# Router products from rows not yet normalised, and expert rows modulated on GpSimd, in a two-layer diffusion backbone

## The chip, the cores and the metric

The kernel runs on one core of a Trainium2 chip. The metric is the device time of one execution in microseconds, the median of several runs. A profiled execution of the kernel before gives the trace that is read here.

## What is computed

Two layers over 512 token rows of 1024 columns: 256 latent tokens and 256 context tokens, which have different modulation vectors. Each layer has three mixers (attention, gated linear attention, neighbourhood attention), merged by gates and an output product, and then a mixture of experts:

```
y  = w_out( sum_i sigmoid(gate_i(h)) * proj_i(branch_i) )
x  = LayerNorm(alpha * x + gate1 * y)
h2 = LN0(x) * (1 + scale2) + shift2
x  = LayerNorm(alpha * x + gate2 * HierMoE(h2))     # top-1 of 4 groups, then top-2 of its 8 experts
```

LN0 takes off a row's mean and divides by its deviation. The router multiplies h2 by a weight of 36 columns (4 for the groups, 32 for the experts) and adds a bias. The chosen experts get the rows of h2 and weight their results by the gates. The last layer needs the latent tokens alone.

## The kernel before

Rows are worked on in tiles of 128 tokens: four in layer 0 (tiles 0 and 1 latent, 2 and 3 context), two in layer 1. A modulation vector so belongs to a pair of tiles, s = t // 2. Products in full precision are put together from a high and a low part of each operand, three products in the place of one (`mm3`, L380 to L382).

`out_norm` ends the mixers. For each tile it makes the output products (PSUM tile wo, 48 products of 512 columns), multiplies them by the gate (L1107), adds them to the residual (L1108) and normalises (`norm1`, L354 and L355). L355 writes the rows x1 and their sums. `norm2` then makes the rows h2 of LN0 (`norm0`: statistics L300, factor by `rsqrt` L276 to L281, the row by ScalarE, L320), and `logits` transposes them (L1151), modulates the transposed tiles while it takes them out of PSUM (half on VectorE, L1159, half on ScalarE, L1157) and multiplies by the router's weight (L1161). `top2` adds the bias (L1200) and picks group and experts by a chain of small operations on 8 or 64 columns, up to the table M (L1223), two tiles at a time. `h2_done` transposes the modulated tiles back into token rows (L1126) and splits them into a high part on ScalarE and a low part on VectorE (L806, L807).

`route` then counts the rows of each expert (cum, rank, row) and makes one-hot matrices OH (L1362), with which `experts` gathers rows (XT, L1384) ahead of the first product with an expert's weight (L1507). Expert weights come as loads of 1 MB (`ew`, L1464). Between the mixers of layer 0 and its experts the modulation vector of layer 1 is also made (`modulation`, L493: sixteen loads of 512 KB named wmod, products L495).

The order on each engine is made by a scheduler that reads the program as written and places instructions by its own estimates; buffers are reused by tag, and a load waits until the last reader of its buffer is done. All loads named here are issued by SyncE (SP), in its order. GpSimd (POOL) does additions of the merge (L1046) and of the experts' results (L1433), and nothing between the two in either layer.

Of the kernel before, what the change touches and what calls it, by code (L numbers as in the profile page):

```python
# [23 lines left out]
EPS = 1e-6  # L24
# [68 lines left out]
HB = (), ()  # L93
LAST = 1, 0
# [12 lines left out]
QS = (2,), ()  # L107
# [142 lines left out]
class _Prog:  # L250
# [220 lines left out]
    def modulation(self, l, groups, tag="raw", tag2="b2", ps="mod"):  # L471
# [12 lines left out]
        for g in groups:  # L484
# [15 lines left out]
            nc.vector.tensor_tensor(mg, p, bm, op=ALU.add)  # L500
            pt = self.ps(ps + "T")
# [8 lines left out]
            for j in range(4):  # L510
                if g == 0:
                    o, plus = self.mT[l][:, 1 - j // 2], j // 2
                elif (g, j // 2) in ((1, 1), (2, 0)):
                    o, plus = self.mT2[l][:, 2 - g], g - 1
                else:
                    continue
# [536 lines left out]
    def out_norm(self, l, T, src):  # L1053
# [44 lines left out]
        for t in range(T):  # L1098
# [20 lines left out]
    def h2_done(self, l, t):  # L1119

        nc = self.nc
        hi, lo = self.t([128, 1024], "h4", F32R, "h2hi"), self.t([128, 1024], "h4", F32R, "h2lo")
        for i in range(2):
            p = self.ps("h2b")
            for k in range(4):
                nc.tensor.transpose(p[:, 128 * k:128 * k + 128], self.h2T[t][:, 4 * i + k], self.ident)  # L1126
            ns = slice(512 * i, 512 * i + 512)
            if t in HB[l]:
                x = self.t([128, 512], "b2", name="h2f")
                nc.scalar.copy(hi[:, ns], p)  # L1130
# [581 lines left out]
```

## Time and profile before

| | us |
|---|---|
| runs (3): median, lowest to highest | 2150.22, 2148.58 to 2153.83 |
| profiled execution, its own time | 2150.77 |
| its span in the trace | 2148.9 |
| TensorE busy in the span | 1973.0 |
| VectorE busy | 964.7 |
| ScalarE busy | 561.5 |
| GpSimd busy | 277.5 |

The span runs from the first to the last instruction; the 1.9 us beside it are start and end. The trace gives each instruction its start and length on its engine: PE is TensorE, DVE VectorE, ACT ScalarE, POOL GpSimd, SP SyncE. A busy TensorE is not one at its peak, since the ends of products are modelled. TensorE's mean granted clock was 0.969 of its full level. What is written behind a row in brackets is the idle time of the engine before it and what ended that.

### The profile page before, as it was taken

Reading aid. Unit: us, or ns where it says so; the run is one execution under the profiler, and the core shown is the slowest. Engines: PE = TensorE matmul, PEld = TensorE weight load, DVE = VectorE, ACT = ScalarE, POOL = GpSimd, SP = SyncE. Lnnn points to the kernel's source line nnn. Section 1 sums busy time; section 2 is a strip of 40 time slices with the busy share of each in tenths; the row PEclk is TensorE's granted clock in tenths of the full one; section 3 lists DMA queues with packets and bytes.
Section 4 is the critical chain, followed back from the end, with each engine's and each line's share of the span. In section 5 each row is a group of like instructions: output and inputs, shape, how many; then the busy total and the mean of one; then the engine's idle time right before and its main releaser. Section 6 shows DMA issues by size and latency. Waiting matters only on the chain. (4 is left out here: it accounts for less than half of the span.)

```text
span 2148.9 us, 28075 instructions
## 1 busy us (share of the span) xinstructions
PE 1973.0 (92%) x10749; PEld 1179.0 (55%) x10749; DVE 964.7 (45%) x2236; ACT 561.5 (26%) x992; POOL 277.5 (13%) x268
## 2 busy tenths in 40 slices
PE   6999999999998898989899598999996999999995
PEld 2676777767885353445253176887795433333331
DVE  4676765554487131222022766776658222221113
ACT  3453344443333000000010254444452111100000
POOL 1322100011100010111011222100020001000000
PEclk9999999999999999999999798999997999999998
DMA  8436222333328999999998723642466999999995
GB/s 300 160 118 220 69 69 70 94 99 120 99 91 321 400 420 420 372 385 420 420 369 367 276 84 116 197 127 85 140 210 253 401 421 422 422 422 422 421 422 224
DMA packets 113987, 562.41 MB, mean 262 GB/s; under 512 B 13302, under 2 KB 14838, under 8 KB 72120
## 3 DMA queue, kind: packets, MB, share of 16 engines
q1 hardware_dynamic: 113272, 558.85, 67.7%
q8 instruction: 87, 1.43, 0.3%
q10 hardware_dynamic: 576, 1.70, 0.2%
q14 instruction: 52, 0.43, 0.1%
HBM read 557.36 MB, written 3.15 MB: 261 GB/s over the span
## 5 line engine op out<-in xcount | busy, mean ns | idle before, releaser
L1507 PE MATMUL h<-ew,XT 128*64 128x512 f32 (+2 forms) x2048 | 479.0, 616 | 39.6 <-DMA ew<-in_ew_dram 39.5
L1507 PEld LDWEIGHTS h<-ew,XT 128*64 128x64 f32 (+2 forms) x2048 | 147.3, 136 | 325.7 <-issue 251.0
L1415 PE MATMUL Y<-ew,aT 128*64 128x512 f32 (+2 forms) x1024 | 250.4, 598 | 10.2 <-DMA ew<-in_ew_dram 7.8
L292 DVE TENSOR_TENSOR wlo<-raw,whi 128x1024 fp32r<-128x1024 f32 (+1 forms) x140 | 179.1, 1279 | 138.0 <-ACT whi L291 136.9
L1433 POOL TENSOR_TENSOR x<-x,ct 128x512 f32<-128x512 f32 x82 | 104.9, 1306 | 996.9 <-DVE ct L1432 873.7
L380 PE MATMUL pT<-hThi,whi 128*128 128x512 f32 (+1 forms) x576 | 204.0, 354 | 2.2 <-DVE zq L869 1.4
L291 ACT CAST whi<-raw 128x1024 fp32r<-128x1024 f32 (+1 forms) x140 | 145.4, 1039 | 223.4 <-PE pT L381 123.8
L382 PE MATMUL pT<-hThi,wlo 128*128 128x512 f32 (+1 forms) x576 | 203.2, 353 | 0.2 <-DVE wlo L292 0.2
L381 PE MATMUL pT<-hTlo,whi 128*128 128x512 f32 (+1 forms) x576 | 202.9, 352 | 0.0
L1404 DVE SCALAR_TENSOR_TENSOR act<-h,s,sl 128x512 f32<-128x512 f32 x30 | 22.5, 751 | 317.6 <-PE h L1507 263.9
L806 ACT CAST Yh<-Y 128x512 fp32r<-128x512 f32 x60 | 35.2, 586 | 467.7 <-PE Y L1415 467.7
L1415 PEld LDWEIGHTS Y<-ew,aT 128*64 128x64 f32 (+2 forms) x1024 | 75.5, 133 | 149.2 <-issue 123.8
L807 DVE TENSOR_TENSOR Yl<-Y,Yh 128x512 fp32r<-128x512 f32 x60 | 41.4, 690 | 252.8 <-ACT Yh L806 249.7
L380 PEld LDWEIGHTS pT<-hThi,whi 128*128 128x128 f32 x576 | 110.7, 192 | 23.8 <-issue 6.0
L382 PEld LDWEIGHTS pT<-hThi,wlo 128*128 128x128 f32 x576 | 110.7, 192 | 16.1 <-issue 2.6
L381 PEld LDWEIGHTS pT<-hTlo,whi 128*128 128x128 f32 x576 | 110.7, 192 | 14.3 <-issue 1.9
L380 PE MATMUL pM<-whi,hThi 128*128 128x512 f32 (+1 forms) x304 | 110.7, 369 | 3.6 <-ACT qTkT L645 1.9
L381 PE MATMUL pM<-wlo,hThi 128*128 128x512 f32 (+1 forms) x304 | 110.9, 365 | 0.0
L382 PE MATMUL pM<-whi,hTlo 128*128 128x512 f32 (+1 forms) x304 | 110.1, 364 | 0.0
L495 PE MATMUL mod<-wmod,sT 128*32 128x512 f32 x320 | 75.2, 636 | 22.5 <-DVE s L341 14.1
L1408 ACT COPY aT<-aT 128x512 f32<-128x512 f32 x30 | 17.6, 585 | 294.4 <-PE aT L1407 294.4
L1384 PE MATMUL XT<-OH,h2hi 128*128 128x256 f32 x352 | 88.6, 289 | 0.2 <-DVE OH L1362 0.2
(364 smaller groups left out, 3088.5 us busy)
## 6 DMA issues: line engine op xcount, KB each, us to landing
ew<-in_ew_dram SPq DMA_DIRECT2D x326, 1024.0 KB, 13.6
raw<-in_w_dram SPq DMA_DIRECT2D x145, 512.0 KB, 3.7
ew<-in_ew_dram SPq DMA_DIRECT2D x116, 512.0 KB, 13.5
wmod<-in_wmod_dram SPq DMA_DIRECT2D x96, 512.0 KB, 6.4
nb<-in_nb_dram SPq DMA_DIRECT2D x32, 256.0 KB, 3.8
g<-md SPq DMA_DIRECT2D x12, 256.0 KB, 7.3
row<-in_ln_dram SPq DMA_DIRECT2D x4, 512.0 KB, 5.3
lgb<-in_ln_dram SPq DMA_DIRECT2D x4, 512.0 KB, 12.2
```

The costliest lines, as they stand in the source:

```text
L291: self.nc.scalar.copy(hi, src)
L292: (eng or self.nc.vector).tensor_tensor(lo, src, hi.bitcast(F32), op=ALU.subtract)
L380: mm(out, lh, rh, start=start, stop=False)
L381: mm(out, lh, rl, start=False, stop=False)
L382: mm(out, ll, rh, start=False, stop=stop)
L495: nc.tensor.matmul(p[32 * j:32 * j + 32, :], self.sT[:, k, :], raws[j // 2][:, 512 * (j % 2):512 * (j % 2) + 512], start=k == 0, stop=k == 7)
L806: self.nc.scalar.copy(hi, src)
L807: self.nc.vector.tensor_tensor(lo, src, hi.bitcast(F32), op=ALU.subtract)
L1384: mm(p[:, w * j:w * j + w], self.h2s[t][part][:, 128 * k:128 * k + 128], OH[:, t], start=t == 0 and part == 0, stop=t == T - 1 and part == 1)
L1415: mm(y[m * i:m * i + m, :], aT[:, 128 * f + m * i:128 * f + m * i + m], w2(f, n, i), start=f == 0, stop=f == 3)
L1433: (nc.vector if last and n else nc.gpsimd).tensor_tensor(self.x1[t][:, ns], self.x1[t][:, ns], tmp, op=ALU.add)
L1507: mm(h[m * i:m * i + m, :], XTs[dp][:, k, 128 * pr + m * i:128 * pr + m * i + m], w[i, 2 * q + k // 4][k % 4], start=k == 0, stop=k == 7)
```

## The change

Four things change.

- `logits` transposes x1 as it is, ahead of the second norm, and takes it out of PSUM by two plain copies. The router's weight is multiplied by 1 + scale2 beforehand (`wrs`, two operations per pair). With mean m and factor r of a row, its logits are r times the product, minus r m times the column sums of wrs, plus the product of shift2 with the weight, plus the bias.
- `router`, a new function at the start of the output stage, makes wrs, the column sums (eight products with ones per pair, L1133) and the products with the shift (eight per pair, L1135). It is called ahead of the loads of the output weights.
- `top2` puts mean and factor in by two operations per tile (L1216, L1217), where one for two tiles added the bias.
- `h2` makes the experts' rows without transposes: four loads per pair bring scale and shift as rows to all partitions (`m2`, L1159), ScalarE squares and sums (L1165) and writes the normalised row (L1170), GpSimd multiplies and adds (L1174, L1175, two halves each), ScalarE writes the high part and GpSimd the low part (L288, L289). `h2_done` is gone. `modulation` stores scale2 with one added.

```diff
         def norm2(t):
             first[t]()
-            h = self.t([128, 1024], "o4", name="h2")
-            self.norm0(self.x1[t], h, total[t] if t in QS[l] else None)
-            self.logits(l, t, h)
-
+            self.logits(l, t, T)
+            self.h2(l, t, total[t])
+
+        self.router(l, T)
...
             norm1(t)
             norm2(t)
-            if t % 2 and t < T - 1:
+            if t % 2:
                 self.top2(l, t - 1, t + 1, T)
-            if t:
-                self.h2_done(l, t - 1)
-        if LAST[l]:
-            self.h2_done(l, T - 1)
-        self.top2(l, T - 2, T, T)
...
+    def router(self, l, T):
...
+        for s in range(T // 2):
+            ws = [self.t([128, 4, 36], "u1", name="wrs") for _ in range(2)]
+            for i in range(2):
+                nc.vector.tensor_tensor(ws[i], wr[:, 144 * i:144 * i + 144].rearrange("p (k e) -> p k e", e=36),
+                                        self.mT2[l][:, 0, s, 4 * i:4 * i + 4][:, :, None].to_broadcast([128, 4, 36]), op=ALU.mult)
+            self.wrs.append([ws[k // 4][:, k % 4] for k in range(8)])
+            o = 144 + 72 * s
+            for k in range(8):
+                mm(self.pl[:, o:o + 36], self.c["one"][:, 0:1].to_broadcast([128, 128]), self.wrs[s][k], start=k == 0, stop=k == 7)
+            for k in range(8):
+                mm(self.pl[:, o + 36:o + 72], self.mT2[l][:, 1, s, k:k + 1].to_broadcast([128, 128]), wr[:, 36 * k:36 * k + 36], start=k == 0, stop=k == 7)
+            nc.vector.tensor_tensor(self.brt[:, s], self.brt[:, s], self.pl[:, o + 36:o + 72], op=ALU.add)
+
+    def logits(self, l, t, T):
...
+            (nc.scalar.copy if i and t < T - 1 else nc.vector.tensor_copy)(xT[:, 4 * i:4 * i + 4], p.rearrange("p (a b) -> p a b", a=4))
         for k in range(8):
-            mm(self.pl[:, 36 * t:36 * t + 36], hT[:, k], self.wr[:, 36 * k:36 * k + 36], start=k == 0, stop=k == 7)
+            mm(self.pl[:, 36 * t:36 * t + 36], xT[:, k], self.wrs[t // 2][k], start=k == 0, stop=k == 7)
+
+    def h2(self, l, t, total):
...
+            for g, j in ((2, 0), (1, 2)):
+                for i in range(2):
+                    r = self.t([128, 512], "u2", name="m2")
+                    nc.sync.dma_start(r, self.md[l, g][32 * (j + i) + t // 2:32 * (j + i) + t // 2 + 1, :].to_broadcast([128, 512]))
+                    self.m2.append(r)
...
+        nc.vector.tensor_scalar(nmu, total, -1.0 / 1024, None, op0=ALU.mult)
+        nc.scalar.activation(h, x, AF.Square, bias=nmu, accum_out=v)
+        nc.vector.tensor_scalar(v, v, 1.0 / 1024, EPS, op0=ALU.mult, op1=ALU.add)
+        r = self.rsqrt(v, 1, st[:, 3:6])
+        nc.vector.tensor_tensor(b, nmu, r, op=ALU.mult)
+        self.rb[t] = r, b
+        nc.scalar.activation(h, x, AF.Identity, bias=b, scale=r)
...
+            nc.gpsimd.tensor_tensor(h[:, ns], h[:, ns], self.m2[i], op=ALU.mult)
+            nc.gpsimd.tensor_tensor(h[:, ns], h[:, ns], self.m2[2 + i], op=ALU.add)
+            self.split(h[:, ns], hi[:, ns], lo[:, ns], nc.gpsimd)
...
-        TT(lg, self.pl[:, 36 * t0:36 * t1].rearrange("p (t e) -> p t e", e=36), row(self.brt, 36), op=ALU.add)
+        for t in range(t0, t1):
+            x, o, (r, b) = self.lg[:, 36 * t:36 * t + 36], 144 + 72 * (t // 2), self.rb[t]
+            STT(x, self.pl[:, o:o + 36], b, self.brt[:, t // 2], op0=ALU.mult, op1=ALU.add)
+            STT(x, self.pl[:, 36 * t:36 * t + 36], r, x, op0=ALU.mult, op1=ALU.add)
```

Three places show how the order moves. First, TensorE of the changed kernel in layer 0, among the output products of tile 2 (wo): xT is tile 0's transposed x1, the source x of the transposes is tile 1's.

```order
L378 MATMUL wo_5584<-g_1055_5232,yh_5131 128x512
L1148 MATMUL logit_5156<-wrs_5157,xT_5330 128x36 x4
L1148 MATMUL logit_5156<-wrs_5158,xT_5330 128x36 x4
L379 MATMUL wo_5584<-g_1054_5231,yl_5132 128x512
L377 MATMUL wo_5584<-g_1060_5243,yh_5135 128x512
L1145 MATMUL h2T_5458<-cst,x_1088_5440 128x128 x4
L1145 MATMUL h2T_5464<-cst,x_1088_5440 128x128 x4
L378 MATMUL wo_5584<-g_1061_5244,yh_5135 128x512
```

Logits of tile 0 and transposes of tile 1 stand inside the output stage; before, tile 0's transposes and two of its logit products stood there, and the rest behind the last output product.

Second, VectorE behind the writing of tile 3's x1 in layer 0, before:

```order
L355 SCALAR_TENSOR_TENSOR x_1122_5698,s_5712<-u_5147,s_5699,row_5206 128x1024
L1208 TENSOR_TENSOR s_5454<-s_5454,s_5456 128x8
L300 BN_STATS s_5716<-x_1122_5698 128x6 x2
L1215 SCALAR_TENSOR_TENSOR route_5445<-s_5454,route_5445 128x64
L1159 TENSOR_SCALAR h2T_5599<-h2T_5600,mU_1098 128x128
L301 BN_AGGR s_5716<-s_5716 128x2
L1218 TENSOR_REDUCE s_5452<-route_5445 128x2
L1159 TENSOR_SCALAR h2T_5599<-h2T_5609,mU_1098 128x128
L302 TENSOR_SCALAR s_5716<-s_5716 128x1
```

and now:

```order
L352 SCALAR_TENSOR_TENSOR x_1132_5739,s_5753<-u_5148,s_5740,row_5255 128x1024
L1258 CAST gdp_5506<-gates_5504 128x2
L1164 TENSOR_SCALAR s_5777<-s_5753 128x1
L1146 COPY xT_5756<-h2T_5757 128x512
L1146 COPY xT_5756<-h2T_5763 128x512
L1166 TENSOR_SCALAR s_5777<-s_5777 128x1
L273 TENSOR_SCALAR s_5777<-s_5777 128x1
L275 TENSOR_SCALAR s_5777<-s_5777 128x1
L277 TENSOR_SCALAR s_5777<-s_5777 128x1
L278 SCALAR_TENSOR_TENSOR s_5777<-s_5777 128x1
```

The selection for tiles 0 and 1 (route) and the modulating evictions of tile 2 that were mixed in are done by then, and the statistics are gone: two copies, mean, factor and then the logits follow x1 directly.

Third, GpSimd in layer 0 from the last addition of the merge on, with the engines that each row waits for (h is the normalised row of a tile, m a scale or shift row, h2hi and h2lo the parts):

```order
L1046 TENSOR_TENSOR y_3202<-y_3202,th_5119 128x512 [waits DVE_49,Pool_49]
L1174 TENSOR_TENSOR h_1081_5360<-h_1081_5360,m_1076_5351 128x512 [waits DMAHW3_49,PE_49,Activation_49]
L1174 TENSOR_TENSOR h_1081_5360<-h_1081_5360,m_1077_5353 128x512 [waits DMAHW4_49]
L1175 TENSOR_TENSOR h_1081_5360<-h_1081_5360,m_1078_5355 128x512 [waits DMAHW6_49,Pool_49]
L1175 TENSOR_TENSOR h_1081_5360<-h_1081_5360,m_1079_5357 128x512 [waits DMAHW0_49,Pool_49]
L1174 TENSOR_TENSOR h_1095_5479<-h_1095_5479,m_1076_5351 128x512 [waits PE_49,Activation_49]
L1174 TENSOR_TENSOR h_1095_5479<-h_1095_5479,m_1077_5353 128x512
L1175 TENSOR_TENSOR h_1095_5479<-h_1095_5479,m_1078_5355 128x512 [waits Pool_49]
L289 TENSOR_TENSOR h2lo_5375<-h_1081_5360,h2hi_5374 128x512 [waits PE_49,Activation_49]
```

Before, the additions of the experts' results (L1433) follow the merge's last addition at once; now 24 operations stand between the two in layer 0, six per tile, and twelve in layer 1.

## Rows read from the trace of the kernel before

**Rows 1.** Stretches: length, busy time per engine (instructions), granted TensorE clock, DMA share, GB/s.

```profile
430.00:640.00 210.00, 209.92 (x970) 162.44 (x971) 116.98 (x212) 73.29 (x118) 26.70 (x18) 1.00 0.32 99
...
685.00:690.00 5.00, 5.00 (x45) 5.00 (x44) 5.00 (x17) 0.59 (x1) 0.00 (x0) 1.00 0.24 93
690.00:695.00 5.00, 5.00 (x42) 3.40 (x42) 4.49 (x18) 1.87 (x2) 0.00 (x0) 1.00 0.00 0
695.00:700.00 5.00, 5.00 (x26) 1.72 (x24) 0.41 (x2) 0.33 (x1) 0.00 (x0) 1.00 0.56 188
...
1690.00:2149.00 459.00, 420.89 (x1896) 159.10 (x1892) 96.81 (x164) 42.54 (x75) 38.89 (x30) 0.99 0.96 398
```

**Rows 2.** Timeline of PE, layer 0: start us, length us, line, operation, tiles.

```profile
641.06 0.39 PE L382 MATMUL wo<-g,yl 128*128 128x512 f32 x1
641.29 1.42 PE L1161 MATMUL logit<-wr,h2T 128*128 128x36 f32 x12
642.55 1.07 PE L1151 MATMUL h2T<-cst,h 128*128 128x128 f32 x8
...
692.51 7.95 PE L1507 MATMUL h<-ew,XT 128*64 128x512 f32 x36
```

**Rows 3.** Timeline of DVE, layer 0.

```profile
652.12 1.28 DVE L355 SCALAR_TENSOR_TENSOR x<-u,s,row 128x1024 f32<-128x1024 f32 x1
...
668.57 0.23 DVE L1200 TENSOR_TENSOR route<-logit,brt 128x72 f32<-128x72 f32 x1 [0.60 <-PE logit L1161]
...
675.56 0.23 DVE L1223 TENSOR_TENSOR M<-route 128x64 bf16<-128x64 f32 x1
```

**Rows 4.** Timeline of DVE, layer 1.

```profile
1657.50 0.23 DVE L1223 TENSOR_TENSOR M<-route 128x64 bf16<-128x64 f32 x1
...
1663.24 0.68 DVE L807 TENSOR_TENSOR h2lo<-h2b,h2hi 128x512 fp32r<-128x512 f32 x1
```

**Rows 5.** Timeline of PE, layer 1.

```profile
1641.10 1.97 PE L1151 MATMUL h2T<-cst,h 128*128 128x128 f32 x8 [10.92 <-ACT h L320]
...
1669.41 2.80 PE L1507 MATMUL h<-ew,XT 128*64 128x512 f32 x12
```

**Rows 6.** Stretches of layer 1.

```profile
1630.00:1655.00 25.00, 11.18 (x57) 10.57 (x57) 19.61 (x69) 9.24 (x15) 0.00 (x0) 0.64 1.01 405
1655.00:1660.00 5.00, 2.22 (x12) 1.42 (x12) 4.62 (x36) 0.40 (x2) 0.00 (x0) 0.50 0.26 103
1660.00:1665.00 5.00, 4.84 (x24) 2.94 (x22) 4.88 (x21) 1.17 (x2) 0.00 (x0) 0.89 0.58 198
```

**Rows 7.** Timeline of POOL, three places of layer 0.

```profile
85.91 1.49 POOL L667 TENSOR_TENSOR EQ<-s,gc 128x512 f32<-128x512 f32 x1
...
130.34 0.61 POOL L725 TENSOR_TENSOR YX<-gc 128x256 f32<-128x256 f32 x1
130.91 0.61 POOL L724 TENSOR_TENSOR YX<-gc 128x256 f32<-128x256 f32 x1
...
563.06 1.29 POOL L1046 TENSOR_TENSOR y<-y,th 128x512 f32<-128x512 f32 x1 [5.03 <-DVE th L1045]
```

**Rows 8.** Timeline of DVE, beside the rows of POOL.

```profile
86.76 0.41 DVE L654 TENSOR_TENSOR r<-pM,brow 128x256 f32<-128x256 f32 x1
...
130.44 0.53 DVE L284 TENSOR_TENSOR s<-s 128x2 f32<-128x2 f32 x1
131.00 0.53 DVE L285 SCALAR_TENSOR_TENSOR s<-s,s 128x2 f32<-128x2 f32 x1
...
134.45 0.16 DVE L285 SCALAR_TENSOR_TENSOR s<-s,s 128x2 f32<-128x2 f32 x1
```

**Rows 9.** Timeline of SP's DMA issues, layer 0.

```profile
639.41 12.18 SPq L493 DMA_DIRECT2D wmod<-in_wmod_dram  x14
```

More of the change, by code (lines that the diff above doesn't have):

```diff
@@ L92 @@
 WARM = 0, 8
-HB = (), ()
-LAST = 1, 0
 NE2 = 4, 3
@@ L106 @@
 FIRST = 0
-QS = (2,), ()
 def groups(l):
@@ L513, in modulation @@
                 elif (g, j // 2) in ((1, 1), (2, 0)):
-                    o, plus = self.mT2[l][:, 2 - g], g - 1
+                    o, plus = self.mT2[l][:, 2 - g], 0
                 else:
@@ L1137, in logits @@
-    def logits(self, l, t, h):
-        nc, mm = self.nc, self.nc.tensor.matmul
-        if t == 0:
-            self.wr = self.t([128, 288], "u2", name="wr")
-            nc.sync.dma_start(self.wr, self.a["wr"][l])
-            self.pl = self.ps("logit")
-            self.h2s, self.h2T = [], []
-        s = t // 2
-        hT = self.t([128, 8, 128], "o4", name="h2T")
-        self.h2T.append(hT)
+    def router(self, l, T):
+        nc, mm = self.nc, self.nc.tensor.matmul
+        wr = self.t([128, 288], "u2", name="wr")
+        nc.sync.dma_start(wr, self.a["wr"][l])
+        self.brt = self.t([128, 2, 36], "u1", name="brt")
+        for s in range(T // 2):
+            nc.sync.dma_start(self.brt[:, s], self.a["brt"][l:l + 1, :].to_broadcast([128, 36]))
+        self.pl = self.ps("logit")
+        self.wrs, self.h2s, self.rb = [], [], {}
+        for s in range(T // 2):
+            ws = [self.t([128, 4, 36], "u1", name="wrs") for _ in range(2)]
[9 more added lines that the diff above has]
+            nc.vector.tensor_tensor(self.brt[:, s], self.brt[:, s], self.pl[:, o + 36:o + 72], op=ALU.add)
@@ L1148, in logits @@
+    def logits(self, l, t, T):
+        nc, mm = self.nc, self.nc.tensor.matmul
+        xT = self.t([128, 8, 128], "o4", name="xT")
         for i in range(2):
@@ L1150, in logits @@
             for k in range(4):
-                nc.tensor.transpose(p[:, 128 * k:128 * k + 128], h[:, 512 * i + 128 * k:512 * i + 128 * k + 128], self.ident)
-            for k in range(4):
-                kt = 4 * i + k
-                o, x = hT[:, kt], p[:, 128 * k:128 * k + 128]
-                scale, shift = (self.mT2[l][:, j, s, kt:kt + 1] for j in range(2))
-                if k % 2:
-                    nc.scalar.activation(o, x, AF.Identity, bias=shift, scale=scale)
-                else:
-                    nc.vector.tensor_scalar(o, x, scale, shift, op0=ALU.mult, op1=ALU.add)
@@ new lines, in h2 @@
+    def h2(self, l, t, total):
+        nc = self.nc
+        if t % 2 == 0:
+            self.m2 = []
+            for g, j in ((2, 0), (1, 2)):
[3 more added lines that the diff above has]
+                    self.m2.append(r)
+        st = self.small(20)
+        nmu, v, b = st[:, 0:1], st[:, 1:2], st[:, 2:3]
+        x, h = self.x1[t], self.t([128, 1024], "o4", name="h2")
+        nc.vector.tensor_scalar(nmu, total, -1.0 / 1024, None, op0=ALU.mult)
[5 more added lines that the diff above has]
+        nc.scalar.activation(h, x, AF.Identity, bias=b, scale=r)
+        hi, lo = self.t([128, 1024], "h4", F32R, "h2hi"), self.t([128, 1024], "h4", F32R, "h2lo")
+        for i in range(2):
+            ns = slice(512 * i, 512 * i + 512)
+            nc.gpsimd.tensor_tensor(h[:, ns], h[:, ns], self.m2[i], op=ALU.mult)
+            nc.gpsimd.tensor_tensor(h[:, ns], h[:, ns], self.m2[2 + i], op=ALU.add)
+            self.split(h[:, ns], hi[:, ns], lo[:, ns], nc.gpsimd)
+        self.h2s.append((hi, lo))
@@ L1663, in run @@
             self.route(l, T)
-            if not LAST[l]:
-                self.h2_done(l, T - 1)
             if l:
```

21 lines of the change are left out of this document (3 added, 18 removed).

## The prediction

> **What bounds the kernel now.** I read the table of stretches first. In layer 0 TensorE works 209.92 of the 210 us before the last output products [rows 1]: what is added to its queue there moves the end of that stage. After it the transfers bound: the queue runs dry at about 686 us and is busy again at about 697. The idle shares of the three rows are 0.76 x 5, 1.00 x 5 and 0.44 x 5 us, together 11.0 us, and from 1690 us on, in layer 1's experts, the DMA engines are 0.96 busy [rows 1]. So in each layer the time after the mixers is set by the moment at which experts start to give weight buffers back, in layer 0 with 11 us of idle transfer time as the most that an earlier start can win.
>
> The timeline of TensorE gives that moment: last output product at 641.06, first expert product at 692.51 [rows 2]. VectorE's timeline shows what stands between: the fourth tile's normalised row x1 is made at 652.12, its logits enter the top-2 selection at 668.57, the table M of chosen experts is made at 675.56 [rows 3]. These 16.45 us are the second norm (statistics, factor, the row written by ScalarE), transposes, modulating evictions, logits, all queued between other work. Layer 1 has the same chain with less around it: TensorE stands idle for 10.92 us until ScalarE has written the first normalised row, M comes at 1657.50, a last split of transposed-back rows at 1663.24, the first expert at 1669.41 [rows 4, 5]. There too the transfers pause: shares 0.26 and 0.58 in the two stretches from 1655, after 1.01 [rows 6].
>
> **The change, part by part.** The sum is made against the profiled execution, 2150.77 us, which lies 0.55 above the median of 2150.22.
>
> *Router products ahead of the output products.* 32 products of 36 columns in layer 0, 16 in layer 1. A product of this shape leaves two records; the twelve records at 641.29 last until the next row at 642.55, 1.26 us, so 0.21 us a product [rows 2]. They stand where TensorE has no gap: 32 x 0.21 = 6.7 us, and 16 x 0.21 = 3.4.
>
> *Transposes and logits of tiles 0 and 1 in layer 0* now stand between output products: 16 transposes and 16 logit products, where there were 8 and 2. Eight transposes take 1.07 us [rows 2], so 1.1 + 14 x 0.21 = 4.0. The last output product of layer 0 moves by 6.7 + 4.0 = 10.7 us to about 652.
>
> *Logits from rows not yet normalised.* From x1 on the chain keeps a transposition (1.1), two plain evictions, eight logit products (1.7), and beside them Square on ScalarE, the factor and the mean. With the writing of x1 itself (1.3) and the two short operations per tile that put factor and mean in, I count 6.5 us where 16.45 were: 10 us less in layer 0. In layer 1 two tiles' statistics, the wait of 10.92 us for ScalarE [rows 5] and the modulating evictions go, but the first norm's own statistics and factor of both tiles, which the order lets run in the same time, stay: I count 4.3 us less up to the logits. The transposes back go too; the last of their splits stands right ahead of the one-hot rows (0.68, at 1663.24) [rows 4], 1.2 with its wait: 5.5 together.
>
> So far layer 0 gives +10.7 - 10 = +0.7, layer 1 +3.4 - 5.5 = -2.1.
>
> *Rows modulated on GpSimd.* Each tile now sends six 128x512 operations with two inputs to GpSimd: 24 in layer 0, 12 in layer 1. Such an operation takes 1.29 us [rows 7]. They run from the second norm of tile 0 to the end of the selection, while GpSimd did nothing there before. VectorE's chain in that time is short dependent operations, and its rows next to a busy GpSimd are the point on which I decide. A 128x2 operation with two inputs lasts 0.53 at 130.44 and again at 131.00, where one of its kind with GpSimd out of the way lasts 0.16 [rows 8]; GpSimd's operations of 0.61 start at 130.34 and 130.91, and each pair ends together [rows 7]. The two engines take turns: the short operation pays for the rest of GpSimd's. An operation with one input in PSUM goes through undisturbed: 0.41 at 86.76, in the middle of GpSimd's 1.49 from 85.91 [rows 7, 8]. The top-2 selection has about 14 operations with both inputs in SBUF up to M, each rsqrt has three. What one GpSimd operation costs the chain lies between 0 (it meets a reduce, a PSUM operand or idle time) and its whole 1.29; I take half, 0.64, the mean rest of an operation met at a random point. Of the 24 I leave out the first four, which meet VectorE while it waits for output products; of layer 1's twelve I leave out three for the logits that VectorE waits for. 20 x 0.64 = 12.8 us and 9 x 0.64 = 5.8 us.
>
> The Trainium skill has this as a rule (SBUF — State Buffer, section "Who interferes with whom"): an operation of VectorE with two inputs in SBUF and one of GpSimd that reads SBUF share a pair of ports, the first to issue holds it for its whole length, and the other is fully blocked. The taking of turns and the free PSUM operand in this trace agree with it. Read at its fullest, with each of the 36 operations met at its start, the rule gives the third rival below instead of my sum.
>
> *Loads.* Four row-broadcast loads of 256 KB per pair of tiles are new. Layer 0's second set waits for GpSimd's first additions of tile 1 and stands ahead of the sixteen wmod loads on SyncE, the first of which is issued at 639.41 now [rows 9]. With the output products 10.7 us later these can't start before about 650, with the wait perhaps at 654. That queue needs some 46 us (639.41 to about 686), so it now lasts until 696 to 700, and the idle 11 us are used up by the delay alone. The loads cost nothing more as long as experts start later than that.
>
> *Sum.* Layer 0: +10.7 - 10 + 12.8 = +13.5, all of it passed on, since experts then start after the transfer queue has run dry. Layer 1: +3.4 - 5.5 + 5.8 = +3.7. Together +17.2: 2150.77 + 17.2 = **2168 us**, by its own uncertainty 2158 to 2180.
>
> **The rivals.** *GpSimd hides.* If its operations meet reduces, PSUM operands and waits, only +0.7 and -2.1 stay: 2149.4, no change that a measurement can tell (about 0.3%, 6.5 us, is what it can). For it: under the output products VectorE has much single-input work. Against it: the selection is almost nothing but two-input operations, and tile 3's rows come just then.
>
> *Faster.* The same, and the router products also cost nothing, because the recorded ends of products are modelled and the stage has slack that "busy" hides. Then layer 0 gets 4.0 - 10 = -6 out of its 11 us of idle transfers and layer 1 -5.5: 2150.77 - 11.5 = 2139.3. It decides if the last output product of layer 0 ends before about 646 and M before 670. Against it: products follow one another every 0.23 us there, with no gap (641.06 to 641.29) [rows 2].
>
> *Much slower.* Every GpSimd operation is met at its start and costs the chain its whole 1.29: 24 x 1.29 = 31.0 and 12 x 1.29 = 15.5, with +0.7 and -2.1: 2150.77 + 45.1 = 2195.9. For it: VectorE is close to full between tile 2's output products and M, so a delay of one tile pushes the next. Against it: fewer than half of its operations there have both inputs in SBUF.
>
> **How the numbers follow.** My forecast 0.55, GpSimd hides 0.22, faster 0.10, much slower 0.13. The range takes in the first two and the near part of the last: 2147 to 2184; outside are the faster case and most of the far one, under 0.2. Faster by over 0.3%: 0.10. Within: 0.22. Slower: 0.55 + 0.13 = 0.68.
>
> **What would show it.** In the changed profile: the last output product of layer 0 near 652, no idle transfers between it and the experts, or a pause later than now; short two-input operations of the selection at 0.5 to 1.4 us instead of 0.16 to 0.23 wherever a GpSimd operation runs; M of layer 0 near 689 and of layer 1 near 1661 plus layer 0's shift. I am wrong if these operations keep their lengths, if M comes no more than 3 us later than 675.56, or if the output products end where they did.

## The result, and the profile after

| | kernel before | changed kernel |
|---|---|---|
| median of the runs, us | 2150.64 (2148.58 to 2153.83) | 2163.85 (2160.37 to 2171.40) |
| ratio, 95% interval | 1 | 1.0064 [1.0046, 1.0082] |
| profiled execution, its own time | 2150.77 | 2171.40 |
| its span | 2148.9 | 2169.6 |

The change costs 13.2 us by the medians. A second set of six runs, beside 22 more of the kernel before, gave 2168.32 against 2152.57, ratio 1.0066 [1.0046, 1.0086]. The profiled execution is the slowest of its five, so its 20.6 us more than the profile of before are split up first.

The table of stretches of the changed kernel, layer 0, then layer 1's experts (columns: stretch, its sum, busy time of each engine, granted clock as a share of full, busy share of the DMA engines, GB/s). It answers [rows 1].

```profile
430.00:640.00 210.00, 210.00 (x1028) 164.72 (x1027) 111.15 (x189) 73.97 (x121) 26.64 (x20) 1.00 0.33 105
640.00:655.00 15.00, 14.53 (x76) 11.98 (x74) 14.39 (x39) 5.38 (x8) 10.61 (x8) 1.00 0.12 39
655.00:680.00 25.00, 16.34 (x99) 8.54 (x100) 23.41 (x77) 9.80 (x15) 14.93 (x13) 0.80 1.00 386
680.00:685.00 5.00, 0.00 (x0) 0.00 (x0) 4.69 (x10) 0.62 (x1) 3.95 (x4) 0.84 1.01 422
685.00:690.00 5.00, 3.25 (x21) 1.18 (x24) 4.03 (x31) 0.90 (x3) 1.27 (x1) 0.50 0.81 293
690.00:695.00 5.00, 3.97 (x20) 2.15 (x12) 4.97 (x32) 0.00 (x0) 0.00 (x0) 0.64 0.91 324
...
700.00:705.00 5.00, 5.00 (x30) 5.00 (x29) 2.68 (x10) 0.00 (x0) 0.00 (x0) 0.61 0.96 376
705.00:710.00 5.00, 5.00 (x51) 4.98 (x52) 1.45 (x3) 1.66 (x3) 0.00 (x0) 1.00 0.12 49
710.00:715.00 5.00, 5.00 (x24) 1.60 (x24) 2.73 (x9) 0.80 (x1) 0.00 (x0) 1.00 0.16 26
...
1690.00:2149.00 459.00, 436.42 (x1999) 168.11 (x1996) 89.89 (x151) 44.73 (x78) 38.10 (x30) 1.00 0.99 411
```

TensorE is as full ahead of the output products as before, and idle where VectorE and GpSimd are both busy (680 to 685). Behind that idle stretch its granted clock is 0.50 from 685 to 690, the lower of its two levels (1.2 GHz in place of 2.4), and it comes back to 1.00 only at 705; before, it was 1.00 from 685 on. The transfers pause at 705 to 715, in place of 686 to 697.

TensorE's timeline of the changed kernel, for [rows 2]: last output product, logits of tile 2, first count product, first gathered rows, first expert product.

```profile
653.26 0.40 PE L379 MATMUL wo<-g,yl 128*128 128x512 f32 x1
661.78 3.63 PE L1148 MATMUL logit<-wrs,xT 128*128 128x36 f32 x16 [7.25 <-DVE xT L1146]
685.89 0.19 PE L1287 MATMUL cum<-M,c_tri 128*128 128x32 bf16 x1 [7.77 <-DVE M L1240]
698.78 0.58 PE L1401 MATMUL XT<-OH,h2hi 128*128 128x256 f32 x1 [4.56 <-DVE OH L1379]
709.83 2.37 PE L1524 MATMUL h<-ew,XT 128*64 128x512 f32 x10
```

Each of the three waits is for VectorE. Its timeline, for [rows 3]: x1 of tile 3, the selection of tiles 2 and 3 up to M, then the slot reduction and the first one-hot row.

```profile
667.58 1.29 DVE L352 SCALAR_TENSOR_TENSOR x<-u,s,row 128x1024 f32<-128x1024 f32 x1
...
668.79 1.23 DVE L1258 CAST gdp<-gates 128x2 bf16<-128x2 f32 x1
...
676.75 0.25 DVE L1216 SCALAR_TENSOR_TENSOR route<-logit,s,brt 128x36 f32<-128x36 f32 x1
...
678.12 0.97 DVE L1225 TENSOR_TENSOR s<-s,s 128x8 f32<-128x8 f32 x1
679.12 1.25 DVE L1232 SCALAR_TENSOR_TENSOR route<-s,route 128x64 f32<-128x64 f32 x1
680.40 0.22 DVE L1235 TENSOR_REDUCE s<-route 128x2 f32<-128x64 f32 x1
680.65 0.93 DVE L1222 TENSOR_TENSOR route<-route,s 128x64 f32<-128x64 f32 x1
681.62 1.19 DVE L1223 TENSOR_TENSOR route<-route,cst 128x64 f32<-128x64 f32 x1
...
684.83 0.22 DVE L1223 TENSOR_TENSOR route<-route,cst 128x64 f32<-128x64 f32 x1
...
685.62 0.22 DVE L1240 TENSOR_TENSOR M<-route 128x64 bf16<-128x64 f32 x1
...
691.36 0.42 DVE L1327 TENSOR_REDUCE r<-route 128x8 f32<-128x256 f32 x1
...
698.25 0.48 DVE L1379 SCALAR_TENSOR_TENSOR OH<-cst,r,O 128x256 fp32r<-128x256 f32 x1
```

GpSimd in the same time:

```profile
677.79 2.49 POOL L1174 TENSOR_TENSOR h<-h,m 128x512 f32<-128x512 f32 x2 [1.62 <-ACT h L1170]
680.24 2.49 POOL L1175 TENSOR_TENSOR h<-h,m 128x512 f32<-128x512 f32 x2
682.68 1.27 POOL L289 TENSOR_TENSOR h2lo<-h,h2hi 128x512 fp32r<-128x512 f32 x1
```

L1223 takes 1.19 us at 681.62, beside GpSimd, and 0.22 at 684.83, behind it. The reduction at 680.40, which has one input, keeps its length beside GpSimd. Operations that read PSUM (L1216) keep theirs too, but they fall between 676.2 and 677.8, where GpSimd waits for ScalarE, so they show nothing here; number 6 does. SyncE, for [rows 9]: the loads of layer 1's modulation start 0.6 us behind the last output product.

```profile
649.96 3.80 SPq L1159 DMA_DIRECT2D m<-md  x3
653.86 15.33 SPq L490 DMA_DIRECT2D wmod<-in_wmod_dram  x14
```

Layer 1, for [rows 4, 5]: last output product at 1650.55, then

```profile
1678.15 0.21 PE L1287 MATMUL cum<-M,c_tri 128*128 128x32 bf16 x1 [11.44 <-DVE M L1240]
...
1689.35 14.00 PE L1524 MATMUL h<-ew,XT 128*64 128x512 f32 x64
```

**Where the 20.7 us of the span came from.** Profiles of these kernels differ by up to 10 us in a stretch that the change hardly touches: the first gate row of layer 0 (th on VectorE, L1045) starts at 448.3 in the profile of before, at 449.81 in this one, at 445.00 in a second profile of the same changed kernel, and between 441.9 and 451.5 in all. So all lengths below run from one instruction to another. Start +1.5; from that row to layer 0's first expert product 244.2 to 260.0, +15.8; router products of layer 1 +3.8; layer 1 from the last output product to the first gathered rows 35.2 to 34.4, -0.8; the rest +0.4.

The lengths in all kernels tried, in us, each the difference of two starts in the kernel's timelines. wo is the last output product, M the second table M (tiles 2 and 3) in layer 0 and the only one in layer 1, OH the first one-hot row, exp the first expert product, th-wo1 from layer 1's first gate row to its first output product, XT the first gathered rows.

| kernel | L0: th-wo | wo-M | M-OH | OH-exp | th-exp | L1: th-wo1 | wo-M | M-XT | XT-end | ratio of the times to before [95%] |
|---|---|---|---|---|---|---|---|---|---|---|
| before | 192.8 | 34.5 | 6.7 | 10.2 | 244.2 | 77.8 | 27.7 | 7.5 | 483.9 | 1 |
| changed | 203.4 | 32.4 | 12.6 | 11.6 | 260.0 | 81.5 | 27.3 | 7.0 | 484.7 | 1.0064 [1.0046, 1.0082] |
| changed, again | 203.5 | 32.4 | 12.6 | 11.9 | 260.4 | 81.9 | 27.3 | 7.0 | 484.6 | 1.0066 [1.0046, 1.0086] |
| 1 no GpSimd | 203.5 | 20.5 | 11.8 | 11.3 | 247.0 | 81.8 | 22.1 | 5.8 | 484.0 | 0.9981 [0.9971, 0.9990] |
| 2 one product | 198.7 | 31.6 | 9.3 | 10.9 | 250.6 | 78.2 | 27.3 | 8.8 | 486.4 | 1.0041 [1.0028, 1.0055] |
| 3 logits only | 203.1 | 36.0 | 6.8 | 10.1 | 256.0 | 81.7 | 28.0 | 7.4 | 485.5 | 1.0072 [1.0058, 1.0085] |
| 4 GpSimd only | 194.2 | 37.1 | 6.9 | 9.9 | 248.1 | 77.7 | 30.4 | 7.2 | 485.2 | 1.0021 [1.0011, 1.0031] |
| 5 sums | 198.3 | 31.6 | 8.9 | 10.3 | 249.1 | 78.2 | 27.3 | 8.8 | 491.1 | 1.0071 [1.0056, 1.0086] |
| 5 again | 198.8 | 31.6 | 9.3 | 11.0 | 250.7 | 78.2 | 27.3 | 8.8 | 491.2 | 1.0068 [1.0052, 1.0084] |
| 6 selection in PSUM | 204.3 | 25.0 | 9.5 | 9.9 | 248.7 | 81.5 | 22.3 | 8.6 | 484.4 | 1.0015 [1.0003, 1.0026] |
| 7 one-hot rows early | 203.5 | 33.2 | 9.3 | 10.7 | 256.6 | 81.6 | 27.3 | 7.4 | 485.3 | 1.0071 [1.0057, 1.0086] |
| 8 sums and PSUM | 198.5 | 27.6 | 9.2 | 10.0 | 245.4 | 78.2 | 22.3 | 10.1 | 490.4 | 1.0018 [1.0006, 1.0030] |
| 8 again | 198.5 | 25.1 | 10.1 | 11.0 | 244.8 | 78.2 | 22.3 | 10.1 | 490.1 | 1.0009 [0.9998, 1.0019] |
| 9 GpSimd only, PSUM | 194.0 | 30.6 | 7.1 | 10.1 | 241.8 | 78.7 | 26.9 | 6.9 | 484.4 | 0.9972 [0.9959, 0.9985] |

The two profiles of the changed kernel agree within 0.4 us in every column. Those of kernels 5 and 8 differ more in layer 0, by up to 1.6 us in th-exp and 2.5 in wo-M, so there differences under 3 us between kernels do not count; in layer 1's columns repeated profiles agree within 0.4. The stretch between (layer 0's first expert product to layer 1's first gate row) is left out: it scatters between 834 and 844 us, and by 4.2 us between the two profiles of kernel 8.

### The profile page after: what moved, and what is told of

The parts are those of the page before. It is cut to its first block, busy times and chain, and to the rows that moved or that the text cites. A ratio compares the mean times of both kernels' runs of the same rounds, so it can differ in the third digit from the quotient of the medians.

```text
span 2169.6 us, 28230 instructions
## 1 busy us (share of the span) xinstructions
PE 1975.0 (91%) x10797; PEld 1184.8 (55%) x10797; DVE 979.5 (45%) x2218; ACT 560.4 (26%) x982; POOL 323.9 (15%) x304
## 5 line engine op out<-in xcount | busy, mean ns | idle before, releaser
L1432 PE MATMUL Y<-ew,aT 128*64 128x512 f32 (+2 forms) x1024 | 250.6, 598 | 11.9 <-DMA ew<-in_ew_dram 9.5
L289 DVE TENSOR_TENSOR wlo<-raw,whi 128x1024 fp32r<-128x1024 f32 (+1 forms) x140 | 180.1, 1287 | 139.6 <-ACT whi L288 138.5
L288 ACT CAST whi<-raw 128x1024 fp32r<-128x1024 f32 (+1 forms) x140 | 145.4, 1038 | 232.1 <-PE pT L378 134.0
L806 ACT CAST Yh<-Y 128x512 fp32r<-128x512 f32 x60 | 35.2, 587 | 468.8 <-PE Y L1432 468.8
## 6 DMA issues: line engine op xcount, KB each, us to landing
ew<-in_ew_dram SPq DMA_DIRECT2D x116, 512.0 KB, 13.5
nb<-in_nb_dram SPq DMA_DIRECT2D x32, 256.0 KB, 3.8
m<-md SPq DMA_DIRECT2D x12, 256.0 KB, 3.8
g<-md SPq DMA_DIRECT2D x12, 256.0 KB, 6.6
```

What stands on the lines that cost most here:

```text
L288: self.nc.scalar.copy(hi, src)
L289: (eng or self.nc.vector).tensor_tensor(lo, src, hi.bitcast(F32), op=ALU.subtract)
L806: self.nc.scalar.copy(hi, src)
L1432: mm(y[m * i:m * i + m, :], aT[:, 128 * f + m * i:128 * f + m * i + m], w2(f, n, i), start=f == 0, stop=f == 3)
```

## The experiments

The theory was that GpSimd and VectorE take turns, and that this and the fuller TensorE queue cost what the shorter chain does not give back. The rivals were that one of the two costs alone counts, and, seen in the timeline above, that the late place of the one-hot rows on VectorE does it (6.9 us lie between slot reduction and first one-hot row, 1.8 before).

**1. GpSimd's operations taken away.**

```diff
-            nc.gpsimd.tensor_tensor(h[:, ns], h[:, ns], self.m2[i], op=ALU.mult)
-            nc.gpsimd.tensor_tensor(h[:, ns], h[:, ns], self.m2[2 + i], op=ALU.add)
-            self.split(h[:, ns], hi[:, ns], lo[:, ns], nc.gpsimd)
+            nc.gpsimd.tensor_tensor(h[:, 512 * i:512 * i + 2], h[:, 512 * i:512 * i + 2], self.m2[i][:, 0:2], op=ALU.mult)
+            nc.gpsimd.tensor_tensor(h[:, 512 * i:512 * i + 2], h[:, 512 * i:512 * i + 2], self.m2[2 + i][:, 0:2], op=ALU.add)
+            nc.scalar.copy(hi[:, ns], h[:, ns])
+            nc.scalar.copy(lo[:, ns], h[:, ns])
```

> GpSimd's multiplications and additions of the experts' rows are cut from 512 columns to 2, and the low part is written by a ScalarE copy in place of GpSimd's subtraction. Left out: the modulation of all columns but 2 in each half, and the true low part, so the experts compute with other rows. Router products, loads and the order of TensorE stay. Theory of turns (GpSimd's operations hold up VectorE's short two-input operations, some 17 us in layer 0 and some 6 in layer 1 by the lengths in the trace of the changed kernel): the selection's operations are back at 0.15 to 0.25 us, M of layer 0 comes at 674 to 679 in place of 685.62, and the time falls by 8 to 18 us to 2146 to 2156. Theory of TensorE's queue (the 12 us by which the output products end later are what counts): M of layer 0 stays above 682 and the time within 3 us of the changed kernel's, 2161 to 2167. Theory of the order (the one-hot rows come late on VectorE whatever GpSimd does): first one-hot row still 12 us behind M in layer 0, and about 5 us of the loss stay.

Measured 2145.98 (2143.84 to 2151.36) beside 2150.60 of the kernel before, 18 us below the changed kernel. From the last output product to M 20.5 us in place of 32.4, in layer 1 22.1 in place of 27.3; the one-hot rows still come 11.8 behind M. VectorE's groups by form between 600 and 720 us (count | busy, mean ns), the changed kernel first:

```profile
L278 DVE SCALAR_TENSOR_TENSOR s<-s 128x1 f32<-128x1 f32 x24 | 6.9, 290 | 0.2
L277 DVE TENSOR_SCALAR s<-s 128x1 f32<-128x1 f32 x24 | 6.4, 268 | 0.3
L1223 DVE TENSOR_TENSOR route<-route,cst 128x64 f32<-128x64 f32 x4 | 2.8, 702 | 0.1
L1232 DVE SCALAR_TENSOR_TENSOR route<-s,route 128x64 f32<-128x64 f32 x2 | 2.5, 1245 | 0.1
L1222 DVE TENSOR_TENSOR route<-route,s 128x64 f32<-128x64 f32 x4 | 2.3, 577 | 0.1
L1225 DVE TENSOR_TENSOR route<-route,s 128x64 f32<-128x64 f32 x4 | 2.3, 572 | 0.1
```

And without GpSimd's work, where the table operations stand one line further down:

```profile
L277 DVE TENSOR_SCALAR s<-s 128x1 f32<-128x1 f32 x24 | 6.4, 268 | 0.3
L278 DVE SCALAR_TENSOR_TENSOR s<-s 128x1 f32<-128x1 f32 x24 | 3.7, 155 | 0.2
L1223 DVE TENSOR_TENSOR route<-route,s 128x64 f32<-128x64 f32 x4 | 0.9, 223 | 0.1
L1224 DVE TENSOR_TENSOR route<-route,cst 128x64 f32<-128x64 f32 x4 | 0.9, 221 | 0.1
L1226 DVE TENSOR_TENSOR route<-route,s 128x64 f32<-128x64 f32 x4 | 0.9, 219 | 0.1
L1233 DVE SCALAR_TENSOR_TENSOR route<-s,route 128x64 f32<-128x64 f32 x2 | 0.5, 250 | 0.1
```

Operations with two tensors in SBUF shrink to between a fifth (L1232) and a half (L278) of their mean length, those of one tensor and two scalars (L277) stay. That GpSimd's work costs the chain up to M 11.9 and 5.3 us is shown (up to the gathered rows of layer 1, 34.4 in place of 27.9, 6.5); the theory of TensorE's queue alone is out. TensorE's granted clock between the last output product and M is 1.00 in this kernel and 0.81 in the changed one, where it stands idle more; how much of the 11.9 comes by way of the clock was not split off.

**2. Router products cut to one of eight.**

```diff
-            for k in range(8):
-                mm(self.pl[:, o:o + 36], self.c["one"][:, 0:1].to_broadcast([128, 128]), self.wrs[s][k], start=k == 0, stop=k == 7)
...
+            mm(self.pl[:, o:o + 36], self.c["one"][:, 0:1].to_broadcast([128, 128]), self.wrs[s][0], start=True, stop=True)
+            mm(self.pl[:, o + 36:o + 72], self.mT2[l][:, 1, s, 0:1].to_broadcast([128, 128]), wr[:, 0:36], start=True, stop=True)
```

> One product in place of eight for each column sum and each shift product of the router: 28 of 32 products less in layer 0, 14 of 16 in layer 1. Left out: seven eighths of these sums, so the logits, and with them the chosen experts, are others. GpSimd's operations stay. The scheduler puts the one-hot rows of layer 0 earlier on VectorE here, close behind the slot reduction, as it did before the change; that part of the difference is read apart. Theory of TensorE's queue: 28 x 0.21 = 5.9 us in layer 0 and 2.9 in layer 1 come off, the last output product of layer 0 ends at about 647.5, time 2153 to 2157. Theory of turns: the last output product ends as early as that, but M of layer 0 comes less than 3 us earlier than 685.62, because VectorE's blocked operations hold it; with the earlier one-hot rows at most 5 us less again: 2156 to 2163. Theory of the order: M as in the changed kernel, first one-hot row 7 to 9 us behind M in place of 12.6, time 2157 to 2160.

Measured 2159.58 (2156.74 to 2161.67). The first output product comes 6.1 us earlier behind the gate row (147.7 for 153.8), the last one 4.8, M 5.5 (wo-M keeps its length), layer 1's 14 products are 3.3. So what TensorE's queue gives passes on to M in full, against what I expected of the theory of turns: the two costs stand one behind the other and add. With the one-hot rows 3.3 earlier layer 0 gains 9.4 us, but the time is only 4.3 below the changed kernel's: M-XT of layer 1 takes 1.8 back, and the long stretch between the layers is 4.6 longer in this profile, hardly more than its scatter between two profiles of one kernel.

**3 and 4. Each half alone.** Logits from x1 with transposed rows (3), and GpSimd's rows with the logits of before (4).

Kernel 3, inside h2:

```diff
-            nc.gpsimd.tensor_tensor(h[:, ns], h[:, ns], self.m2[i], op=ALU.mult)
...
+                nc.tensor.transpose(p[:, 128 * k:128 * k + 128], h[:, 512 * i + 128 * k:512 * i + 128 * k + 128], self.ident)
...
+                nc.tensor.transpose(p[:, 128 * k:128 * k + 128], hT[:, 4 * i + k], self.ident)
+            self.split2(p, hi[:, ns], lo[:, ns])
```

Kernel 4, inside norm2, with logits as it was before the change and h2 without its statistics:

```diff
-            self.logits(l, t, T)
-            self.h2(l, t, total[t])
+            h = self.t([128, 1024], "o4", name="h2")
+            self.norm0(self.x1[t], h, total[t])
+            self.logits(l, t, h)
+            self.h2(l, t, h)
```

> One half of the change alone: logits from rows not yet normalised with the router products on TensorE; the experts' rows go through transposes, modulating evictions and transposes back, as before the change. Nothing is left out. No GpSimd operation and no row loads between the mixers and the experts. Theory of turns: no two-input operation of the selection above 0.3 us, M of layer 0 at 672 to 679 although the output products end at 653 or later, time 2145 to 2157. Theory of TensorE's queue: the router products and the later end of the output products cost what they cost in the changed kernel, and transposes come on top: 2160 to 2168.

> The other half alone: logits from normalised, modulated, transposed rows as before the change, no router products; the experts' rows are modulated on GpSimd with the row loads. Nothing is left out. Theory of turns: the last output product of layer 0 ends near 643 to 645, but the two-input operations of the selection last 0.5 to 1.3 us, M of layer 0 comes 8 to 14 us later than the 675.56 of the kernel before, and the time is 2158 to 2172. Theory of TensorE's queue: M near 675, time 2147 to 2154.

Measured: 3 is at 2166.78 (2161.06 to 2171.03), 4 at 2155.71 (2150.67 to 2158.81). On 3 the theory of turns missed and the time is the one that the theory of TensorE's queue gave (2160 to 2168). The selection operations are short again, but x1 of tile 3 is written at 661.14 and its transposes start only here (TensorE of kernel 3):

```profile
673.58 1.05 PE L492 MATMUL mod<-wmod,sT 128*32 128x512 f32 x4
674.56 0.44 PE L1182 MATMUL h2b<-cst,hU 128*128 128x128 f32 x2
674.93 1.05 PE L492 MATMUL mod<-wmod,sT 128*32 128x512 f32 x4
675.91 0.88 PE L1182 MATMUL h2b<-cst,hU 128*128 128x128 f32 x6
676.62 0.60 PE L1145 MATMUL h2T<-cst,x 128*128 128x128 f32 x4
```

Tile 2's transposes back (h2b) and products of layer 1's modulation stand ahead of them, so the selection waits for TensorE. Early logits are worth something only if the rows' transposes leave the queue as well; taking them out is the half of the change that GpSimd pays for. This rests on the one kernel, which makes more transposes than the kernel before and the changed one. 4 lies between the two theories: M comes 2.6 and 2.7 us later behind the last output product than before the change (34.5 to 37.1, 27.7 to 30.4), and in layer 0 4.0 behind the gate row, not 8 to 14. I had given no credit for the transposes back that GpSimd's rows take off the queues, which no run measures alone; number 9 shows what the turns cost in it.

**5. The router's sums on VectorE,** one product with ones for each: all of the computation, but 4 products in layer 0 in place of 32.

```diff
...
+                    nc.vector.tensor_reduce(q[:, i], ms.rearrange("p k e -> p e k"), axis=AX.X, op=ALU.add)
+                nc.vector.tensor_tensor(q[:, 0], q[:, 0], q[:, 1], op=ALU.add)
+                mm(self.pl[:, o + c0:o + c0 + 36], self.c["one"][:, 0:1].to_broadcast([128, 128]), q[:, 0], start=True, stop=True)
```

> The router's column sums and shift products are first summed over k on VectorE, and one product with ones for each is left on TensorE: 4 products in layer 0 in place of 32, 2 in layer 1 in place of 16. Nothing is left out. The one-hot rows stand early on VectorE here. If the router products cost what the first runs say, measured from the first gate row of layer 0 (th, 449.81 in the changed kernel), the first output product of layer 0 comes 5.5 to 6.5 us earlier than in the changed kernel (153.8 behind that row), the first expert product 8 to 10 us earlier (5 of TensorE's queue, 3 to 5 of the order), and the time is 2153 to 2160. If VectorE's blocked operations set the end whatever TensorE does: first expert product at most 5 us earlier, 2158 to 2163.

Measured 2168.41 (2165.33 to 2170.71) beside 2153.53 of the kernel before, no better than the changed kernel. Yet the lengths up to layer 0's experts are as expected or a little better (first expert product 10.9 us earlier, 9.3 in a second profile). What is lost stands in the last stretch, 491.1 for 484.7. So the changed kernel, this one and number 8 were run once more.

> The changed kernel itself, beside two of the earlier kernels on one chip: a second set of runs to measure the others against, and a second profile. If its profile was late by chance before layer 1 (the first gate row at 449.81, other profiles between 442.71 and 451.50), this one differs by that alone: layer 0 from the first gate row to the first expert product again 260, last output product of layer 1 to the first gathered rows (XT) again 34.4. Ratio to the kernel before 1.004 to 1.008.

> The kernel with the router's sums on VectorE again. Its first expert product of layer 0 came 10.9 us earlier than the changed kernel's, and its time was no better. Two explanations. Chance: its experts of layer 1 ran at 416 GB/s in that profile where most have 420 to 421, about 5 us over 190 MB, and the rest is scatter; then it is 4 to 8 us faster than the changed kernel beside it. Transfers: the earlier start is given back in the experts' loads of both layers, whatever the run; then it is within 2.5 us of the changed kernel, its rate in layer 1 is 416 again, and its last experts of layer 0 come at most 7 us earlier than the changed kernel's.

> The kernel with the sums on VectorE and the selection in PSUM again. By chance: 420 GB/s in layer 1 this time, ratio to the kernel before 0.998 to 1.001. By the transfers: 416 GB/s again, ratio 1.001 to 1.003.

Measured 2168.32 (2161.07 to 2172.94), 2168.30 (2161.77 to 2171.84) and 2155.07 (2152.38 to 2158.39). The table of stretches for layer 1's experts, 1700 to 2000 us, of the changed kernel:

```profile
1700.00:2000.00 300.00, 290.79 (x1378) 116.75 (x1376) 64.63 (x109) 30.36 (x54) 26.41 (x20) 1.00 1.02 421
```

And of kernel 5, in its second profile:

```profile
1700.00:2000.00 300.00, 287.02 (x1328) 111.00 (x1324) 62.12 (x102) 29.90 (x53) 26.24 (x20) 1.00 1.02 417
```

The DMA engines are as busy, but move 417 GB/s. So it is in this stretch in all four profiles of kernels 5 and 8, and 421 or 422 in the other ten. The 484 us of the last stretch are nearly all transfers, and 1% of them is 5 us of the 6.5 lost. So it is not chance, and it is the transfers, though by another way than I wrote: their rate, not their start. Kernel 2, with as few products, ran at 422, so it is not the products. What kernels 5 and 8 have in common beside the sums is 864 bytes more per partition of small tiles (one tile of 4 x 36 and one of 2 x 36 numbers of 4 bytes); that this moves the weight buffers to places where loads are slower was not tried and stays open.

**6. The selection's tables in PSUM,** with GpSimd's work as in the changed kernel.

```diff
-            self.lg, self.oh = x[:, 0:144], x[:, 144:400]
+            self.tl, self.lg, self.oh = x[:, 0:144], self.pl[:, 0:144], x[:, 144:400]
...
+            self.el = self.pl[:, 288:416]
...
+            z = self.pl[:, 416:416 + n * w].rearrange("p (t e) -> p t e", e=w)
...
-                nc.vector.scalar_tensor_tensor(y, b, 1.5, y, op0=ALU.add, op1=ALU.mult)
+                nc.vector.tensor_scalar(y, b, 1.5, y, op0=ALU.add, op1=ALU.mult)
```

> All of the changed kernel's GpSimd operations stay. The tables of the top-2 selection lie in free columns of the logits' PSUM tile, so that each of its two-input operations but the last (M) has one operand in PSUM; the factor's two-input operations become operations of one tensor and scalars. Nothing is left out. The one-hot rows stand early on VectorE here. Theory that the two engines take turns for operands in SBUF: the selection's operations last 0.2 to 0.3 us beside GpSimd's 1.3 in place of 0.9 to 1.25; from the last output product to M of layer 0 22 to 25 us pass in place of 32.4, in layer 1 22 to 25 in place of 27.3; with 3 to 5 us of the order the time falls by 15 to 22 us, to 2142 to 2149. Rival, that any GpSimd work slows VectorE, wherever the operands lie (or that the order alone did it): the operations stay at 0.5 us and above, M as late as in the changed kernel, time 2157 to 2162.

Measured 2155.78 (2153.44 to 2161.80) beside 2153.53, ratio 1.0015 for 1.0064: about 10.5 us of the loss gone. From the last output product to M 25.0 and 22.3 us, as the theory of turns had it. VectorE's timeline in this kernel, layer 0, tiles 2 and 3:

```profile
673.28 0.23 DVE L1225 TENSOR_TENSOR logit<-logit,s 128x64 f32<-128x64 f32 x1
673.55 0.23 DVE L1226 TENSOR_TENSOR logit<-logit,cst 128x64 f32<-128x64 f32 x1
...
675.90 1.03 DVE L1243 TENSOR_TENSOR M<-route 128x64 bf16<-128x64 f32 x1
```

And GpSimd's:

```profile
671.90 2.50 POOL L1174 TENSOR_TENSOR h<-h,m 128x512 f32<-128x512 f32 x2 [3.11 <-ACT h L1170]
674.34 2.51 POOL L1175 TENSOR_TENSOR h<-h,m 128x512 f32<-128x512 f32 x2
676.79 2.51 POOL L289 TENSOR_TENSOR h2lo<-h,h2hi 128x512 fp32r<-128x512 f32 x2
```

Beside the same operations of GpSimd, a table operation with one operand in PSUM takes 0.23, and M, the last of the selection and with both in SBUF, 1.03. That separates the place of the operands from GpSimd's being busy. The time fell less than the 15 to 22 expected: 11.3 us by layer 0's first expert product, 3.5 by layer 1's first gathered rows, while the stretch between was 3.3 longer in this profile, which is within its scatter.

**7. The one-hot rows early,** by a change of one operation at the kernel's start that tips the scheduler.

```diff
-                nc.vector.tensor_scalar(mg[0:64], mg[0:64], 1.0, None, op0=ALU.add)
+                nc.scalar.activation(mg[0:64], mg[0:64], AF.Copy, bias=1.0)
```

> One addition of 1 to the modulation rows at the kernel's start goes to ScalarE in place of VectorE. Nothing is left out. Its cost is nothing, but the scheduler then puts the first one-hot rows of layer 0 six instructions behind the slot reduction on VectorE, in place of twenty-two behind it. Theory of the order: M of layer 0 as late as in the changed kernel (measured from the first gate row, 235.8), first one-hot row 6.5 to 9 us behind M in place of 12.6, time 3 to 6 us less, 2158 to 2161. Rival (the transfers or TensorE's second half of the rows hide it): time within 1.5 us of the changed kernel's, 2162 to 2166.

Measured 2167.56 (2166.10 to 2172.35) beside 2153.53, ratio 1.0071. The one-hot rows came 3.3 us earlier, the experts 3.4, and no gain is seen in the time, though one of 3 us would lie within the intervals. The theory of the order holds for the place; for the time it stays open, and it is no large part of the loss.

**8. Sums and PSUM together.**

> Both: the sums on VectorE with one product each, and the selection's tables in PSUM. Nothing is left out. If the router products and the taking of turns are two costs that add, the time is that of the selection in PSUM less 5 to 9 us, 2134 to 2144, faster than the kernel before (2150.6). If one hides the other, it is within 3 us of the better of the two.

Measured 2157.64 (2152.39 to 2163.09) and 2155.07, ratios 1.0018 and 1.0009, within 3 us of kernel 6, not 5 to 9 us below it. By the time alone one cost hides the other; the lengths say something else. Layer 0 has only 1 us left of its loss (th-exp 245.4 and 244.8); the last stretch gives the gain back, as in 5.

**9. A version that is faster than both:** kernel 4 with the selection in PSUM.

> The experts' rows modulated on GpSimd, logits as before the change, and the selection's tables in PSUM. Nothing is left out. Theory of turns: the operations of the selection are back at 0.2 to 0.3 us, M of layer 0 comes 2 to 5 us earlier than without PSUM (231.3 behind the first gate row), M of layer 1 22 to 28 us behind the last output product in place of 30.4, and with no router products ahead of the output products the time is 3 to 9 us below that of the same kernel without PSUM, ratio 0.998 to 1.001 in place of 1.0021. Rival (VectorE is slowed wherever the operands lie): ratio 1.002 or more.

Measured 2147.14 (2142.26 to 2150.17) beside 2152.57, ratio 0.9972 [0.9959, 0.9985] for 1.0021 of kernel 4: some 10 us, a little more than expected. The first expert product comes 2.4 us earlier behind the gate row than before the change, which is no more than two profiles of one kernel differ by, and M of layer 1 0.8. M of layer 0 came 6.7 us earlier behind the gate row than in kernel 4 (th-wo and wo-M together 224.6 for 231.3). The diff to kernel 4 has the lines of number 6.

## Why the prediction was right

**TensorE's queue** (+10.7 in layer 0, +3.4 in layer 1): the last output product came 10.7 us later behind the gate row, 7.1 of it ahead of the first one (6.7 forecast); 3.8 in layer 1. Right in both terms.

**The chain without GpSimd** (-10 in layer 0, -5.5 in layer 1): kernel 1 shows it alone. 34.5 became 20.5, -14.0, and layer 1 from last output product to gathered rows 35.2 became 27.9, -7.3. The prediction had sized it 4 and 2 us too small.

**GpSimd's rows** (+12.8 and +5.8, half an operation's 1.29 us for each of 20 and 9): 11.9 up to M and, up to the gathered rows, 6.5 by the difference of the changed kernel to kernel 1. The sums are near, but not by the count that made them. In layer 0, from x1 of tile 2 to M, the timeline has 17 operations of VectorE that last 0.36 to 1.08 us longer beside GpSimd than the shortest of their kind in the profiles of the kernel before and of kernel 1, 14.0 us together: 17 meetings of 0.82 us, where the prediction had 20 of 0.64. That the two errors nearly cancel is luck. The rule of the Trainium skill that stood beside it (SBUF — State Buffer, section "Who interferes with whom") agrees in its condition, both inputs in SBUF, with number 6; its fullest reading, each operation paid whole, would have been 31 and 15.5, and isn't what happened: the 24 and 12 operations cost 11.9 and 6.5, within the range between 0 and 1.29 for each.

**The loads:** wmod started at 653.86 (650 to 654 forecast), and the pause of the transfers moved behind it to 705 to 715. A later pause was foreseen; the transfers ran until 705, where 696 to 700 was forecast.

**What I did not foresee:** M to the first one-hot row, 6.7 to 12.6 us, and 1.3 more to the experts. The order on VectorE behind M was not among the places I read; the additions for modulation, copies of slot rows and a second set of flags stand ahead of the one-hot rows there. Number 7 ties 3.3 of these 5.9 us to the order, and at most 0.9 is GpSimd's (number 1); the rest is not split up. The 1.3 are TensorE's clock, for which the prediction had no term: the 64 products that gather the first rows follow one another every 0.21 us at the low level and every 0.12 at the full one, 9 of the 63 steps were slow before and 23 are now, and 14 x 0.09 = 1.3. By chance all this made up for what the chain gave beyond my count: up to M layer 0 came to +10.7 - 14.0 + 11.9 = +8.6, where +13.5 was forecast, and as a whole to +10.7 - 14.0 + 11.9 + 7.2 = +15.8, against +13.5 forecast, layer 1 to 3.8 - 0.8 = +3.0 against +3.7. M of layer 0 was at 685.62, 1.5 of it the later start (forecast 689), M of layer 1 at 1677.87 (1661 and layer 0's shift, 1678).

**The rivals:** "GpSimd hides" fell with the lengths of 0.93 to 1.25 us, "faster" with the last output product at 653.26 in place of 646, "much slower" with the 11.9 in place of 31. The step "all of it passed on" holds less well than the rest: the sum in the profile is 19.2 us without the start, the medians say 13.2 and 15.7, and kernels 5, 7 and 8 show 3 to 11 us of layer 0 that don't arrive in the time.

## What to carry to other kernels

When work goes to an idle GpSimd, look at what VectorE does in the same time: a chain of small operations with both tensors in SBUF pays up to a whole GpSimd operation for each of them. Putting one of the operands in free PSUM columns, or writing a two-tensor operation as one tensor and scalars (where the second has one number a row), costs 0.01 to 0.05 us an operation and takes the wait away; with it the half of this change that is about GpSimd became a gain. Earlier logits need more products ahead of a stage that is already full: here 10.7 us in layer 0 and 3.8 in layer 1, against 14.0 and 7.3 that the chain gave back with the rows' transposes gone (kernel 1). With the transposes kept (kernel 3) they were a loss.

## What the runs showed of the hardware

- A cast of 128x2 from fp32 to bf16, one input, also waits for GpSimd: 1.23 us at 668.79, 1.18 to 1.24 in twelve such cases over the profiles, each begun behind the start of a GpSimd operation, 0.14 to 0.17 otherwise. I had counted operations of one input as free.
- An operation of one tensor with two scalars from SBUF (L277) keeps its 0.27 us beside GpSimd (four times in the changed kernel, 641.40 to 674.99), while the next operation with two tensors (L278) takes 0.88 there: here scalars did not count as a second input.
- The same loads at the same busy share of the DMA engines ran at 417 GB/s in two kernels and at 421 or 422 in the others, profile after profile; why stays open.
- The first 450 us, which the change hardly touches, differ by up to 9.6 us between profiles (441.9 to 451.5; 4.8 between two of the same kernel), more than most effects looked for here. Lengths between two named instructions are the way around it.
